# Weight sums of a Strassen product moved from GpSimd into accumulating 1 MB DMAs, with other orders of the seven products

## The chip, the cores and the metric

The kernel runs on one core of a Trainium2 chip. A core has five engines with an instruction queue each: TensorE (PE in the rows, PEld for its weight loads), VectorE (DVE), ScalarE (ACT), GpSimd (POOL) and SyncE (SP). They work at the same time and wait for one another on semaphores; each takes its own instructions in order. SP, ACT and POOL also issue DMAs, which 16 DMA engines carry out. Matmul results go to PSUM, eight banks of 128 x 512 floats; everything else lives in SBUF. The metric is the time of one execution on the device, in microseconds.

## The reference

One layer of a hybrid backbone over 1024 latent tokens and 256 context tokens of width 1024. A token mixer (long convolution, gated linear attention, gated delta net) ends in an output projection, and a squared-ReLU MLP follows:

```python
y, yc = mixer(h, hc, rows, with_ctx_out, w_in[l], w_out[l], ...)   # ends in ... @ w_out
x = x + g1 * y
x = x + g2 * sq_relu_mlp(modulate(x, norm2_g[l], sh2, sc2), w_mlp1[l], w_mlp2[l])

def sq_relu_mlp(h, w1, w2):
    return jnp.square(jax.nn.relu(h @ w1)) @ w2
```

Here w_out is 1024 x 1024, w1 1024 x 4096 and w2 4096 x 1024, all float32. A last RMSNorm gives the output.

## The kernel before

The change concerns the last part of the program: the product with w_out and the MLP, whose 4096 inner columns are worked in four quarters g, each a product with a quarter of w1 and one with a quarter of w2. That makes nine products of 1024 x 1024 weights with 1024 tokens. I call each a stage; they follow one another as w_out, w1 (g = 0), w2 (g = 0), w1 (g = 1) and so on. The stages are numbered 0 to 8, so the odd ones are w1, the even ones from 2 on are w2.

Each stage (`stage`) is one step of Strassen's scheme in Winograd's form: weights and tokens are cut into 2 x 2 blocks of 512, and seven products of blocks replace eight. The products have numbers, and `order` gives their order: (1, 5, 2, 6, 7, 4, 3) for w_out and (1, 2, 6, 7, 4, 5, 3) for the MLP. Weight blocks a11, a12, a21, a22 are combined by `weights`: a11 - a21 (product 7), a21 + a22 (5), their combinations with a11 and a12 (6 and 3). Token blocks b11 to b22 are combined by `in_place` (w_out, w2, whose inputs may be overwritten) and `apart` (w1, whose input is needed again).

Float32 operands are split into a high part that TensorE takes at full rate and a low rest (`split`): a cast on ACT makes the high part, a subtraction the low one. `operand` does that for weights into tiles S (four buffers, low part on POOL) and for tokens into tiles T (ten buffers, low part on DVE). Each matmul of operands is three matmuls (`mm3`): 4 parts p x 4 blocks k x 3 = 48 per product and 336 per stage.

Products that share a term accumulate in one PSUM bank: 6, 7 and 4 go on from 1, and 3 from 5 where 3 comes last. Before the next of them may add to a bank, `take` has read it: for w_out and w2, DVE adds the bank times a gate to x1 (the `x` tiles, `adder`); for w1, ACT and DVE form the squared ReLU in tiles `ar` (`up`).

The weights of a stage come by 16 SP transfers of 256 KB into 16 tiles `wr` that are used again stage after stage. POOL makes four sums of 128 x 512 for each p, 16 a stage.

The engines' orders are made when the program is built, by a scheduler that takes the order of the code as priority; what they are is shown below for the places that matter.

Of the kernel before, what the change touches and what calls it, by code (L numbers as in the profile page):

```python
# [119 lines left out]
def layout(x, c, ctx, c_ctx, norm1_g, norm2_g, w_mod, b_mod, w_in, w_out, hy_conv_w, hy_conv_b, hy_f_w1, hy_f_b1, hy_f_w2, hy_f_b2,  # L120
# [16 lines left out]
    A["wout"] = np.ascontiguousarray(w_out[0].reshape(8, 128, 8, 128).transpose(2, 1, 0, 3)).reshape(8, 128, 1024)  # L137
    A["w1"] = np.ascontiguousarray(w_mlp1[0].reshape(8, 128, 32, 128).transpose(2, 1, 0, 3)).reshape(32, 128, 1024)
    A["w2"] = np.ascontiguousarray(w_mlp2[0].reshape(4, 8, 128, 8, 128).transpose(0, 3, 2, 1, 4)).reshape(4, 8, 128, 1024)
# [64 lines left out]
FINAL_AT = (5, 1)  # L204
# [3 lines left out]
class Build:  # L208
# [99 lines left out]
    def run(self):  # L308
        tc, nc = self.tc, self.nc
        self._cst, self.y, self.nT = {}, [], 0  # L310
# [148 lines left out]
    def mod_rest(self, psum, pool):  # L459

        for g in (1, 2):
            yield from self.mod_group(g, psum, "psd", pool, ("mw", "mw"))
        self.stt(self.A2, self.modT[:, 32:40, 0], 1.0, self.vec("n2"), ADD, MUL)
        self.show("modT", self.modT)
        yield
# [997 lines left out]
    def weights(self, srcs):  # L1463

        gp = self.nc.gpsimd
        a = {}
# [7 lines left out]
        done = set()  # L1474

        def get(i, p):
            a11, a12, a21, a22 = [a[p, r, c] for r in range(2) for c in range(2)]
            if i > 4 and p not in done:
                done.add(p)
                self.tt(a11, a11, a21, SUB, gp)  # L1480
                self.tt(a21, a21, a22, ADD, gp)
            src = {1: a11, 2: a12, 3: a12, 4: a22, 5: a21, 7: a11}.get(i)
            if i == 6:
                src = self.temp()
                self.tt(src, a22, a11, SUB, gp)
                self.tt(a12, a12, src, SUB, gp)
            return self.operand(self.W, "S", 4, src, gp)
        return get, lambda: load(1)

    def stage(self, srcs, order, moving, take, after=None, last=None, first=None):  # L1490


        w, rest = self.weights(srcs)
        T = {}
        paired = order[-2:] == (5, 3)
# [9 lines left out]
        rest()  # L1505
        held = {}

        def bank(i, p):

            into = (1 if i in (6, 7, 4) else 5 if i == 3 and paired else i), p  # L1510
# [4 lines left out]
        for n, i in enumerate(order):  # L1515
            if last and n == 6:

                s = [w(i, p) for p in range(4)]
                for j in range(2):
                    c = slice(256 * j, 256 * j + 256)  # L1520
                    for p in range(4):
# [4 lines left out]
                        take(i, p, ps, c)  # L1526
                        if (j, p) == LAST_AT:
                            last(slice(0, 256))
                last(c)
                break  # L1530
            for p in range(4):
# [5 lines left out]
                take(i, p, ps)  # L1537
                if p == 1 and n < 6:
                    sums(order[n + 1])
# [3 lines left out]
    def in_place(self, h, early5=False):  # L1543

        def moving(i, k):
            b11, b12, b21, b22 = h(k, 0), h(k, 1), h(k + 4, 0), h(k + 4, 1)
            if i == 5 and early5:
                t = self.temp()
                self.tt(t, b12, b11, SUB)
                return t  # L1550
            if i == 6:
                self.tt(b12, b22, b12, SUB)
                self.tt(b11, b12, b11, ADD)
            elif i == 4:
                self.tt(b21, b21, b11, SUB)
            elif i == 5:
                self.tt(b12, b22, b11, SUB)
# [3 lines left out]
    def apart(self, h):  # L1561
# [3 lines left out]
        def moving(i, k):  # L1565
            b11, t3, b21, b22 = h(k, 0), h(k, 1), h(k + 4, 0), h(k + 4, 1)
            if i == 6:
                T2[k] = self.M.tile([128, 512], F32, name="u", bufs=4)
                self.tt(T2[k], t3, b11, ADD)
                return T2[k]  # L1570
            if i in (4, 5):
                t = self.temp()
                self.tt(t, b21 if i == 4 else b22, T2[k], SUB)
                return t
            return {1: b11, 2: b21, 3: b22, 7: t3}[i]
        return moving

    def adder(self, gate, acc=None, paired=True):
# [22 lines left out]
        def take(i, p, ps, s=slice(0, 512)):  # L1601
# [10 lines left out]
            elif i == 4:  # L1612
                add(ps, n, 0)
                full(n, 0)
# [24 lines left out]
    def w_out(self):  # L1639
        nc, M = self.nc, self.M  # L1640

        def load():
            self.x1 = [M.tile([128, L], F32, name=f"x1_{k}") for k in range(8)]
            for m in range(8):
# [3 lines left out]
        W = self.I["wout"]  # L1648
        self.stage([(W[p], W[p + 4]) for p in range(4)], (1, 5, 2, 6, 7, 4, 3), self.in_place(y, True), self.adder(16, self.acc, False),
                   (*NORM_AT, lambda: self.norm2(0)), None, load)  # L1650
# [32 lines left out]
    def mlp(self):  # L1683
        nc, M, x1 = self.nc, self.M, self.x1
        h = lambda k, c: self.H[k][:, 512 * c:512 * c + 512]
        order = (1, 2, 6, 7, 4, 5, 3)
        for g in range(4):
            b = {}
            new = lambda: M.tile([128, 512], F32, name="ar", bufs=16)

            def square(o, ps):

                self.act(o, ps, AF.Relu)
                self.stt(o, ps, 0.0, o, MAX, MUL)

            def up(i, p, ps):
                n = p + 4
                at = {1: (p, 0), 6: (p, 1), 7: (n, 1), 4: (n, 0)}.get(i)
                if at:
                    b[at] = new()  # L1700
                if i in (1, 6, 7):
                    nc.scalar.copy(b[at], ps)
                elif i == 4:
                    square(b[at], ps)
                elif i == 5:
                    self.tt(b[n, 1], b[n, 1], ps, ADD)
                    self.act(b[n, 1], b[n, 1], AF.Relu)
                    self.act(b[n, 1], b[n, 1], AF.Square)
                else:
                    o = b[p, 0] if i == 2 else b[p, 1]  # L1710
                    self.tt(ps, o, ps, ADD)
                    square(o, ps)
            W = self.I["w1"]
# [20 lines left out]
```

## Time and profile before

| | us |
|---|---|
| median of three runs | 1757.75 (1752.26 to 1757.88) |
| the profiled execution | 1746.09 |
| its span, first to last instruction | 1744.3 |
| of it TensorE busy | 1545.1 (89%) |
| VectorE busy | 1334.2 (76%) |
| GpSimd busy | 907.7 (52%) |
| ScalarE busy | 808.1 (46%) |

A busy share is an average over a program with many kinds of stages. PEclk is the share of the full 2.4 GHz that TensorE was granted; its lower level is 1.2 GHz. A wait is put down to the instruction whose semaphore came last. Times in the rows count from the span's start.

### The profile page before, as it was taken

The numbers are of one execution on the slowest core, as the hardware profiler recorded it, in microseconds if no ns is written. First come the engines' busy times: TensorE is split into PE (matmuls) and PEld (weight loads), VectorE is DVE, ScalarE is ACT, GpSimd is POOL, SyncE is SP. The second block draws the span as 40 slices with busy tenths as digits, with TensorE's granted clock in tenths as the row PEclk, the third lists the DMA queues.
The fourth block names the chain that finished last, engine by engine and source line by source line (L and its number), as shares of the span: only waits on it lengthen the run. The fifth ranks groups of instructions, "written<-read, shape, count | busy, mean of one in ns | idle before, by whom it ended". The sixth has DMA issues, their size and how long they took to land.

```text
span 1744.3 us, 26573 instructions
## 1 busy us (share of the span) xinstructions
PE 1545.1 (89%) x10096; PEld 1233.0 (71%) x10096; DVE 1334.2 (76%) x1820; ACT 808.1 (46%) x1468; POOL 907.7 (52%) x606
## 2 busy tenths in 40 slices
PE   7899999999999987587887997979998998899887
PEld 2487877776787766487875775768776877687766
DVE  5944597985663866879878788885898589858886
ACT  5432223245656445346542474534543454345444
POOL 0311232415244301627445695877886788678864
PEclk9999999999998977788898998989998999899988
DMA  8333876655675313345365101111111111111002
GB/s 282 123 103 117 300 287 221 226 192 182 184 217 163 127 44 111 90 155 156 108 209 188 60 14 55 43 42 55 55 42 45 53 59 39 48 49 64 34 0 97
DMA packets 123511, 202.31 MB, mean 116 GB/s; under 512 B 29943, under 2 KB 75431, under 8 KB 120696
## 3 DMA queue, kind: packets, MB, share of 16 engines
q1 hardware_dynamic: 99048, 154.45, 26.7%
q10 hardware_dynamic: 19712, 24.14, 4.5%
q0 software_dynamic: 4624, 22.02, 3.8%
q8 instruction: 80, 1.31, 0.3%
q14 instruction: 47, 0.39, 0.1%
HBM read 158.83 MB, written 41.75 MB: 115 GB/s over the span
## 4 chain that ended last, share of the span: by engine, by line
PE 28%; DVE 24%; POOL 4%; issue 3%; ACT 3%; DMA 2%; SPq 1%; POOLq 0%; ACTq 0%; DVEq 0%
PE psb L220 22%; DVE T L248 7%; DVE ar L248 5%; PE pss L220 2%; PE psl L220 2%; DVE lv L248 2%; DVE x L256 2%; POOL S L248 1%; DVE h L248 1%; DVE s L248 1%; DVE bd L248 1%; PE psi L220 1%; POOL wr L248 1%; DVE ar L256 1%; DMA h<-dy 1%
## 5 line engine op out<-in xcount | busy, mean ns | idle before, releaser
L220 PE MATMUL psb<-T,S 128*128 128x512 f32 (+1 forms) x3072 | 726.7, 398 | 80.8 <-ACT S L288 37.1
L220 PEld LDWEIGHTS psb<-T,S 128*128 128x128 f32 x3072 | 585.2, 194 | 220.5 <-ACT S L288 46.7
L248 POOL TENSOR_TENSOR S<-wr,S 128x512 fp32r<-128x512 f32 x216 | 322.8, 1500 | 183.4 <-ACT S L288 182.6
L288 ACT CAST S<-wr 128x512 fp32r<-128x512 f32 x216 | 133.2, 621 | 135.2 <-PE psb L220 115.5
L220 PE MATMUL psb<-ahi,wh 128*128 128x512 f32 x448 | 183.2, 410 | 9.1 <-DVE acc L256 4.8
L220 PE MATMUL psb<-alo,wh 128*128 128x512 f32 x448 | 181.9, 406 | 0.0
L220 PE MATMUL psb<-ahi,wl 128*128 128x512 f32 x448 | 181.0, 404 | 0.0
L248 POOL TENSOR_TENSOR wl<-ws,wh 128x1024 fp32r<-128x1024 f32 x28 | 71.1, 2539 | 206.4 <-ACT wh L288 140.8
L256 DVE SCALAR_TENSOR_TENSOR x<-psb,modT,x 128x512 f32<-128x512 f32 (+1 forms) x148 | 106.1, 727 | 57.3 <-PE psb L220 56.2
L248 DVE TENSOR_TENSOR T<-ar,T 128x512 fp32r<-128x512 f32 x112 | 135.7, 1234 | 17.6 <-ACT T L288 17.5
L256 DVE SCALAR_TENSOR_TENSOR acc<-psb,vecs,acc 128x504 f32<-128x504 f32 (+5 forms) x168 | 111.3, 678 | 49.0 <-ACT acc L260 46.7
L248 POOL TENSOR_TENSOR wr<-wr 128x512 f32<-128x512 f32 x72 | 113.7, 1581 | 12.8 <-DMA wr<-in_wout 12.2
L220 PEld LDWEIGHTS psb<-ahi,wh 128*128 128x128 f32 x448 | 87.1, 195 | 39.3 <-issue 9.1
L248 DVE TENSOR_TENSOR T<-h,T 128x512 fp32r<-128x512 f32 x88 | 107.6, 1251 | 7.8 <-ACT T L288 7.8
L288 ACT CAST T<-ar 128x512 fp32r<-128x512 f32 x112 | 68.5, 618 | 97.1 <-DVE ar L248 52.6
L220 PEld LDWEIGHTS psb<-alo,wh 128*128 128x128 f32 x448 | 87.2, 195 | 25.6 <-issue 7.8
L220 PEld LDWEIGHTS psb<-ahi,wl 128*128 128x128 f32 x448 | 87.2, 195 | 22.3 <-issue 5.1
L248 DVE TENSOR_TENSOR ar<-ar 128x512 f32<-128x512 f32 x64 | 93.2, 1471 | 0.3
L248 POOL TENSOR_TENSOR bd<-lv,qT 64x1024 f32<-64x1024 f32 x16 | 48.7, 3047 | 44.1 <-PE pss L220 32.4
L288 ACT CAST T<-h 128x512 fp32r<-128x512 f32 x88 | 53.4, 618 | 18.4 <-PE psb L220 11.4
L248 POOL TENSOR_TENSOR S<-s,S 128x512 fp32r<-128x512 f32 x36 | 55.4, 1549 | 11.9 <-ACT S L288 11.9
L248 POOL TENSOR_TENSOR s<-wr 128x512 f32<-128x512 f32 x36 | 59.5, 1663 | 1.9 <-DVE T L248 1.9
(330 smaller groups left out, 2809.5 us busy)
## 6 DMA issues: line engine op xcount, KB each, us to landing
wr<-in_w SPq DMA_DIRECT2D x128, 256.0 KB, 2.6
mw<-in_wmod SPq DMA_DIRECT2D x32, 512.0 KB, 5.2
ws<-in_win SPq DMA_DIRECT2D x28, 512.0 KB, 4.1
dft<-in_fw POOLq DMA_DIRECT2D x8, 1024.0 KB, 5.9
dft<-in_iv POOLq DMA_DIRECT2D x8, 1024.0 KB, 6.4
kq<-dKQ SPq DMA_DIRECT2D x64, 96.0 KB, 2.7
wl<-in_wmod SPq DMA_DIRECT2D x8, 512.0 KB, 3.8
wh<-in_wmod SPq DMA_DIRECT2D x8, 512.0 KB, 4.4
```

The costliest lines, as they stand in the source:

```text
L220: return self.nc.tensor.matmul(out, lhsT=lhsT, rhs=rhs, start=start, stop=stop, skip_group_check=more)
L248: return (eng or self.nc.vector).tensor_tensor(out, a, b, op)
L256: return (eng or self.nc.vector).scalar_tensor_tensor(out, a, s, b, op0=op0, op1=op1)
L288: self.nc.scalar.copy(hi, src)
```

## The change

A weight block is now a quarter of the stage's weights in one piece: 128 x 2048 floats, 1 MB, laid out so in device memory. A tile holds a whole block and serves all four p. Sums of blocks are made by issuing a second DMA from POOL into the same tile with `accum_op=ADD`, so that the transfer adds. Such a DMA can only add; therefore the second block row of the result is computed with its sign turned, which makes every weight sum a plain addition (a11 + a21, a21 + a22, a11 + a21 + a22, a11 + a12 + a21 + a22), and the sign comes back in the gates (a multiplication by -1 in `mod_rest`), in the ReLU's scale and in the token sums (`minus`). Transfers cannot subtract again, so a tile only gains blocks: `PLANS` says which blocks go into which of a stage's four or five tiles, with the products that use it in between. The tiles stand in four rooms of 1 MB, each given to the tile whose room was free first (`rooms`).

The order of the MLP's products becomes (1, 5, 6, 3, 2, 7, 4), O1, in the stages of g = 1 to 3; g = 0 keeps its order, O2, and w_out its own, O3. Since 4 now comes last in the last stage, the two final norms swap halves.

```diff
-FINAL_AT = (5, 1)
+FINAL_AT = (4, 1)
+O1, O2, O3 = (1, 5, 6, 3, 2, 7, 4), (1, 2, 6, 7, 4, 5, 3), (1, 5, 2, 6, 7, 4, 3)
+PLANS = {O1: (((0, 0), 1, (1, 0), 7), ((1, 0), (1, 1), 5, (0, 0), (0, 1), 3), ((1, 0), (1, 1), (0, 0), 6), ((0, 1), 2), ((1, 1), 4)),
...
-        def load(j):
-            for i in (j, 1 - j):
-                for p in range(4):
-                    a[p, i, j] = (self.W, self.M)[j].tile([128, 512], F32, name="wr", bufs=8)
-                    self.nc.sync.dma_start(a[p, i, j], srcs[p][i][:, 512 * j:512 * j + 512])
-        load(0)
...
+        def further(t):
+            while todo[t] and not isinstance(todo[t][0], int):
+                i, j = todo[t].pop(0)
+                if t in tiles:
+                    gp.dma_start(tiles[t], src[:, i, j, :], accum_op=ADD)
+                else:
+                    used = base + order.index([x for x in PLANS[order][t] if isinstance(x, int)][-1])
+                    room = min(self.rooms, key=self.rooms.get)
+                    self.rooms[room] = used
+                    tiles[t] = (self.W if room < 2 else self.M).tile([128, 2048], F32, name=f"wr{room}", bufs=1)
+                    self.nc.sync.dma_start(tiles[t], src[:, i, j, :])
+            if todo[t]:
+                at[todo[t].pop(0)] = t
+        def begin(n):
+            for t in sorted(range(5), key=lambda t: order.index(first(t))):
+                if t < len(todo) and t not in tiles and order.index(first(t)) <= n:
+                    further(t)
...
         def get(i, p):
-            a11, a12, a21, a22 = [a[p, r, c] for r in range(2) for c in range(2)]
-            if i > 4 and p not in done:
-                done.add(p)
-                self.tt(a11, a11, a21, SUB, gp)
-                self.tt(a21, a21, a22, ADD, gp)
-            src = {1: a11, 2: a12, 3: a12, 4: a22, 5: a21, 7: a11}.get(i)
-            if i == 6:
-                src = self.temp()
-                self.tt(src, a22, a11, SUB, gp)
-                self.tt(a12, a12, src, SUB, gp)
-            return self.operand(self.W, "S", 4, src, gp)
+            return self.operand(self.W, "S", 4, tiles[at[i]][:, 512 * p:512 * p + 512], gp)
...
+        begin_w(1 if first else 0)
         sums(order[0])
...
         for n, i in enumerate(order):
+            begin_w(n + 2)
...
                 take(i, p, ps)
+                if p == 3:
+                    used(i)
                 if p == 1 and n < 6:
                     sums(order[n + 1])
...
+            if order == O1:
+                if i == 5:
+                    self.tt(b11, b11, b12, SUB)
+                elif i == 6:
+                    self.minus(b11, b11, b22)
+                elif i == 7:
+                    self.tt(b12, b22, b12, SUB)
+                elif i == 4:
+                    self.minus(b21, b11, b21)
+                return {1: b11, 5: b11, 6: b11, 3: b22, 2: b21, 7: b12, 4: b21}[i]
...
-            if i == 6:
-                T2[k] = self.M.tile([128, 512], F32, name="u", bufs=4)
-                self.tt(T2[k], t3, b11, ADD)
-                return T2[k]
+            if i in (4, 5, 6) and k not in T2:
+                T2[k] = self.minus(self.M.tile([128, 512], F32, name="u", bufs=4), t3, b11)
             if i in (4, 5):
-                t = self.temp()
-                self.tt(t, b21 if i == 4 else b22, T2[k], SUB)
-                return t
+                return self.minus(self.temp(), T2[k], b21 if i == 4 else b22)
```

The engines' orders show what moves. On POOL, in the first half of stage 4 (w2, g = 1), before: `wr_115..` and `wr_116..` are quarter blocks, `s_...` is a temporary, and the S rows are low parts.

```order
L248 TENSOR_TENSOR S_11630<-wr_11586,S_11630 128x512
L248 TENSOR_TENSOR wr_11586<-wr_11586,wr_11594 128x512
L248 TENSOR_TENSOR S_11647<-wr_11588,S_11647 128x512
L248 TENSOR_TENSOR wr_11594<-wr_11594,wr_11614 128x512
L248 TENSOR_TENSOR s_11800<-wr_11614,wr_11586 128x512
L248 TENSOR_TENSOR wr_11588<-wr_11588,wr_11596 128x512
L248 TENSOR_TENSOR S_11676<-wr_11590,S_11676 128x512
L248 TENSOR_TENSOR wr_11596<-wr_11596,wr_11616 128x512
```

In the same place of the changed program POOL's queue reads as follows, `wr_11438` being the tile of products 1 and 7, `wr_11452` that of 5 and 3, `wr_11455` that of 6; DMASW and DMAHW are landings of DMAs issued by POOL and by SP.

```order
L255 TENSOR_TENSOR S<-wr_11438,S 128x512 [waits DMAHW5_49,PE_49,Activation_49]
L255 TENSOR_TENSOR S<-wr_11438,S 128x512 [waits PE_49,Activation_49] x3
L1487 DMA wr_11438<-in_w 128x2048 [waits Pool_49]
L255 TENSOR_TENSOR S<-wr_11452,S 128x512 [waits DMASW5_49,Activation_49]
L255 TENSOR_TENSOR S<-wr_11452,S 128x512 [waits Activation_49] x3
L1487 DMA wr_11452<-in_w 128x2048 [waits Pool_49]
L255 TENSOR_TENSOR S<-wr_11455,S 128x512 [waits DMASW7_49,Activation_49]
L255 TENSOR_TENSOR S<-wr_11455,S 128x512 [waits Activation_49]
L1487 DMA wr_11452<-in_w 128x2048 [waits DMASW1_49]
L255 TENSOR_TENSOR S<-wr_11455,S 128x512 [waits Activation_49] x2
L255 TENSOR_TENSOR S<-wr_11452,S 128x512 [waits DMASW2_49,Activation_49]
```

The sums between the low parts are gone; in their place stand DMA issues, of which the second into `wr_11452` waits for the landing of the first, and product 3's first low part for the landing of the second.

On DVE at the border of stage 3 (w1) and stage 4 (w2), before: `x1_...<-psb` rows are the adds of product 1, the rows of `ar` from `ar` alone token sums for product 6, the T row a low part for product 6.

```order
L256 SCALAR_TENSOR_TENSOR x1_0_8914<-psb_11633,modT_156,x1_0_8914 128x512
L256 SCALAR_TENSOR_TENSOR ar_11244<-psb_11498,ar_11244 128x512
L248 TENSOR_TENSOR ar_11030<-ar_11222,ar_11030 128x512
L256 SCALAR_TENSOR_TENSOR x1_1_8915<-psb_11650,modT_156,x1_1_8915 128x512
L248 TENSOR_TENSOR ar_11244<-ar_11332,ar_11244 128x512
L248 TENSOR_TENSOR ar_11405<-ar_11405,ar_11030 128x512
L248 TENSOR_TENSOR ar_11048<-ar_11244,ar_11048 128x512
L256 SCALAR_TENSOR_TENSOR x1_2_8916<-psb_11679,modT_156,x1_2_8916 128x512
L248 TENSOR_TENSOR ar_11423<-ar_11423,ar_11048 128x512
L248 TENSOR_TENSOR T2_11756<-ar_11030,T2_11756 128x512
```

The same border in the changed program, where T8 and T9 belong to product 5 and T0 to T3 to product 6:

```order
L255 TENSOR_TENSOR T8_11502<-ar_10911,T8_11502 128x512
L255 TENSOR_TENSOR T9_11506<-ar_10929,T9_11506 128x512
L263 SCALAR_TENSOR_TENSOR ar_10911<-ar_10911,ar_10996 128x512
L255 TENSOR_TENSOR T0_11579<-ar_10847,T0_11579 128x512
L263 SCALAR_TENSOR_TENSOR ar_10929<-ar_10929,ar_11014 128x512
L263 SCALAR_TENSOR_TENSOR ar_11435<-psb_10916,ar_11435 128x512
L255 TENSOR_TENSOR T1_11583<-ar_10865,T1_11583 128x512
L263 SCALAR_TENSOR_TENSOR x1_0_8905<-psb_11462,modT_156,x1_0_8905 128x512
L263 SCALAR_TENSOR_TENSOR x1_1_8906<-psb_11479,modT_156,x1_1_8906 128x512
L263 SCALAR_TENSOR_TENSOR x1_2_8907<-psb_11512,modT_156,x1_2_8907 128x512
```

The token sums now stand ahead of product 1's adds, not among them.

## Rows read from the trace of the kernel before

**Rows 1.** The core's span in us and its mean granted TensorE clock.

```profile
core 0: 1744.3 us, clock 0.933
```

**Rows 2.** Stages: length, busy of PE, PEld, DVE, ACT, POOL; clock, DMA, GB/s.

```profile
916.80:1018.00 101.20, 86.33 (x355) 69.31 (x354) 82.03 (x96) 41.73 (x73) 65.33 (x43) 0.91 0.30 109
1018.00:1114.30 96.30, 82.80 (x354) 65.51 (x353) 83.96 (x89) 61.00 (x108) 69.63 (x47) 0.95 0.14 44
1114.30:1207.40 93.10, 82.24 (x338) 66.07 (x337) 74.38 (x74) 35.49 (x60) 68.21 (x46) 0.93 0.14 45
...
1286.40:1380.90 94.50, 81.89 (x338) 65.33 (x337) 75.23 (x76) 35.47 (x60) 69.06 (x46) 0.95 0.13 45
1380.90:1460.10 79.20, 77.03 (x338) 62.73 (x337) 63.67 (x62) 46.02 (x85) 65.50 (x44) 1.00 0.17 54
...
1633.90:1731.40 97.50, 85.57 (x404) 70.75 (x402) 81.29 (x94) 43.84 (x78) 64.58 (x43) 0.93 0.06 22
1731.40:1744.30 12.90, 2.75 (x15) 2.19 (x14) 5.24 (x14) 1.64 (x6) 4.19 (x6) 0.59 0.48 163
```

**Rows 3.** Timeline of TensorE in stage 5: start, length, what, idle before.

```profile
1414.39 47.88 PE L220 MATMUL psb<-T,S 128*128 128x512 f32 x209 [0.82 <-ACT S L288]
```

**Rows 4.** Timeline of TensorE in the first half of stage 4.

```profile
1310.16 15.72 PE L220 MATMUL psb<-T,S 128*128 128x512 f32 x60 [4.76 <-ACT S L288]
1332.38 9.85 PE L220 MATMUL psb<-T,S 128*128 128x512 f32 x31 [6.50 <-DVE x L256]
```

**Rows 5.** Chain of waits from 1280 to 1345 us, summed by line.

```profile
by line: DVE ar L248 35.3%; DVE T L248 29.8%; PE psb L220 19.7%; DVE x L256 9.2%; DVE ar L256 3.8%; DVE psb L248 3.7%; ACT ar L260 0.9%; issue 0.4%
```

**Rows 6.** Busy times from 1280 to 1332 us, columns as in rows 2.

```profile
1280.00:1332.00 52.00, 39.77 (x163) 30.74 (x161) 51.27 (x46) 16.89 (x30) 50.87 (x31) 0.96 0.05 16
```

**Rows 7.** DVE and ACT on `ar`: count, then shortest, median, longest ns.

```profile
L248 DVE TENSOR_TENSOR T<-ar,T x112: 677/1217/1785, 1093.5 to 1707.6; 128x512 fp32r<-128x512 f32 x112
...
L256 DVE SCALAR_TENSOR_TENSOR ar<-psb,ar x48: 672/678/693, 1053.3 to 1647.5; 128x512 f32<-128x512 f32 x48
```

**Rows 8.** DVE groups, 1280 to 1332 us: count, busy us, mean ns, idle.

```profile
L248 DVE TENSOR_TENSOR ar<-ar 128x512 f32<-128x512 f32 x16 | 23.8, 1501 | 0.1
L248 DVE TENSOR_TENSOR T<-ar,T 128x512 fp32r<-128x512 f32 x13 | 20.1, 1563 | 0.0
```

**Rows 9.** POOL's weight sums, whole run, columns as in rows 8.

```profile
L248 POOL TENSOR_TENSOR wr<-wr 128x512 f32<-128x512 f32 x72 | 113.7, 1581 | 12.8 <-DMA wr<-in_wout 12.2
...
L248 POOL TENSOR_TENSOR s<-wr 128x512 f32<-128x512 f32 x36 | 59.5, 1663 | 1.9 <-DVE T L248 1.9
L248 POOL TENSOR_TENSOR wr<-wr,s 128x512 f32<-128x512 f32 x36 | 57.8, 1608 | 0.0
```

**Rows 10.** 1 MB loads issued by POOL: issue ns; us to landing.

```profile
L1365 POOL DMA_DIRECT2D dft<-in_fw x8: 528/554/583, 191.8 to 299.6; - x8
...
DMA to landing us min/median/max: 5.0/6.0/12.6
```

**Rows 11.** Groups on POOL from 1280 to 1332 us.

```profile
L248 POOL TENSOR_TENSOR wr<-wr 128x512 f32<-128x512 f32 x8 | 13.6, 1696 | 0.1
L248 POOL TENSOR_TENSOR s<-wr 128x512 f32<-128x512 f32 x4 | 6.9, 1746 | 0.0
L248 POOL TENSOR_TENSOR wr<-wr,s 128x512 f32<-128x512 f32 x4 | 6.9, 1731 | 0.0
```

**Rows 12.** Timeline of POOL in stage 0.

```profile
923.38 1.45 POOL L248 TENSOR_TENSOR wr<-wr 128x512 f32<-128x512 f32 x1 [10.31 <-DMA wr<-in_wout]
```

**Rows 13.** Timeline of TensorE in stage 0.

```profile
932.65 14.28 PE L220 MATMUL psb<-T,S 128*128 128x512 f32 x48 [4.05 <-ACT S L288]
```

**Rows 14.** The casts and low parts of S: shortest, median, longest ns.

```profile
L288 ACT CAST S<-wr x216: 602/622/647, 896.3 to 1721.6; 128x512 fp32r<-128x512 f32 x108
L248 POOL TENSOR_TENSOR S<-wr,S x216: 1260/1398/1832, 897.0 to 1722.3; 128x512 fp32r<-128x512 f32 x108
```

More of the change, by code (lines that the diff above doesn't have):

```diff
@@ L309, in run @@
         tc, nc = self.tc, self.nc
-        self._cst, self.y, self.nT = {}, [], 0
+        self._cst, self.y, self.nT, self.nS, self.rooms = {}, [], 0, 0, {i: i - 9 for i in range(4)}
         with ExitStack() as es:
@@ L1461, in temp, with weights @@
         return self.M.tile([128, 512], F32, name="s", bufs=2)
[L1463 removed]
+    def weights(self, src, order):
         gp = self.nc.gpsimd
[L1466 to L1488 removed]
@@ L1490, in stage @@
-    def stage(self, srcs, order, moving, take, after=None, last=None, first=None):
-        w, rest = self.weights(srcs)
+        at, todo, tiles = {}, [list(t) for t in PLANS[order]], {}
+        base = 8 * self.nS
+        self.nS += 1
+        def further(t):
[11 more added lines that the diff above has]
+                at[todo[t].pop(0)] = t
@@ new lines, in begin, with first @@
+        def begin(n):
+            for t in sorted(range(5), key=lambda t: order.index(first(t))):
+                if t < len(todo) and t not in tiles and order.index(first(t)) <= n:
+                    further(t)
+        def first(t):
+            return next(x for x in PLANS[order][t] if isinstance(x, int)) if t < len(todo) else order[0]
+        def get(i, p):
+            return self.operand(self.W, "S", 4, tiles[at[i]][:, 512 * p:512 * p + 512], gp)
+        return get, begin, lambda i: further(at[i])
@@ L1494, in stage @@
+    def stage(self, src, order, moving, take, after=None, last=None, first=None):
+        w, begin_w, used = self.weights(src, order)
         T = {}
-        paired = order[-2:] == (5, 3)
         def sums(i):
@@ L1504, in stage @@
             first()
-        rest()
         held = {}
         def bank(i, p):
-            into = (1 if i in (6, 7, 4) else 5 if i == 3 and paired else i), p
+            into = (1 if i in (6, 7, 4) else 5 if i == 3 and order != O3 else i), p
             begin = into not in held
@@ L1526, in stage @@
                         take(i, p, ps, c)
+                        if after and j == 0 and (i, p) == after[:2]:
+                            after[2]()
                         if (j, p) == LAST_AT:
@@ L1541, in stage, with minus, in_place @@
                     after[2]()
-    def in_place(self, h, early5=False):
+    def minus(self, out, a, b):
+        self.stt(out, a, -1.0, b, MUL, SUB)
+        return out
+    def in_place(self, h, order):
         def moving(i, k):
             b11, b12, b21, b22 = h(k, 0), h(k, 1), h(k + 4, 0), h(k + 4, 1)
-            if i == 5 and early5:
+            if order == O1:
[8 more added lines that the diff above has]
+                return {1: b11, 5: b11, 6: b11, 3: b22, 2: b21, 7: b12, 4: b21}[i]
+            if i == 5 and order == O3:
                 t = self.temp()
-                self.tt(t, b12, b11, SUB)
+                self.tt(t, b11, b12, SUB)
                 return t
@@ L1612, in take @@
             elif i == 4:
-                add(ps, n, 0)
-                full(n, 0)
+                add(ps, n, 0, s)
+                full(n, 0, s)
             elif i == 5:
@@ L1647, in w_out @@
         y = lambda k, c: self.y[k][:, 512 * c:512 * c + 512]
-        W = self.I["wout"]
-        self.stage([(W[p], W[p + 4]) for p in range(4)], (1, 5, 2, 6, 7, 4, 3), self.in_place(y, True), self.adder(16, self.acc, False),
-                   (*NORM_AT, lambda: self.norm2(0)), None, load)
+        self.stage(self.I["wout"][0], O3, self.in_place(y, O3), self.adder(16, self.acc, False), (*NORM_AT, lambda: self.norm2(0)), None, load)
     def norm2(self, c):
```

57 lines of the change are left out of this document (31 added, 26 removed).

## The prediction

> **What bounds the kernel now.** I read the clock and span first [rows 1], then a table of busy time by stage, then the chain of waits and the instruction groups in the worst stretch, last the DMA landings. The last 827.5 us of the span are nine matrix products (w_out, then w1 and w2 four times), each in seven Strassen products; I cut them at every 336th matmul into T and S. The reader should see in [rows 2] two kinds of stage: a w1 stage lasts 79.2 us with the clock at 1.00 (2.4 GHz), a w2 stage 93.1 to 97.5 us at 0.93 to 0.95. An undisturbed run of 209 matmuls takes 47.88 us [rows 3], 0.229 us each, so a product of 48 costs 11.0 us and a stage 77. The first two stages, 101.2 and 96.3 us, have troubles of their own. All the rest of the program (the first 917 us) keeps its order but for neighbours that swap.
>
> The 15.3 us by which a w2 stage (94.5) exceeds a w1 stage are two idle gaps of TensorE, 4.76 and 6.50 us, one ended by a cast of S on ACT, one by an x add on DVE [rows 4], and some 5 us more of busy time (81.9 against 77.0) under the lower clock. In the stretch of those gaps the chain of waits lies 82% on DVE (35.3 + 29.8 + 9.2 + 3.8 + 3.7) [rows 5]. There, in 52 us, DVE is busy 51.27 us with 46 instructions and POOL 50.87 us with 31 [rows 6]. DVE is slow, not only full: a TENSOR_TENSOR with both operands in SBUF takes 0.677 us at best, 1.217 in the median and 1.785 at worst, while the form with one operand in PSUM takes 0.672 to 0.693 whatever POOL does [rows 7]; in the stretch the 29 SBUF ones average 1.50 and 1.56 us [rows 8]. Two-operand SBUF work on DVE and work on POOL take turns.
>
> **The change, part by part.**
>
> *POOL's sums go.* 72 + 36 + 36 instructions of 1.58 to 1.66 us, 231 us of POOL in all [rows 9], are replaced by 50 accumulating transfers (4 + 2 x 5 + 6 x 6). POOL issues 1 MB loads already, in 0.53 to 0.58 us [rows 10]: 50 x 0.57 = 28 us, hidden by what went. In the 52 us stretch 8 + 4 + 4 = 16 of POOL's 31 instructions are such sums [rows 11], 15 remain. If each remaining one holds up one DVE instruction by 0.85 us (1.53 - 0.68), DVE needs 29 x 0.68 + 17 x 0.70 + 15 x 0.85 = 44.4 us; bounds are 51.3 (every instruction still slow) and 31.6 (none). TensorE needs 163 x 0.229 = 37.3 for its matmuls there, so relief alone gives 6.9 us and leaves 7.1.
>
> *Order of the products.* DVE's work is the same in number: 16 sums in a w2 stage, 12 in a w1 stage, now partly SCALAR_TENSOR_TENSOR, whose row reads 0.678 with one PSUM operand [rows 7]; with two SBUF operands I take the same 0.68, and if POOL slows it as it does the others that is already in the 0.85. In the order 1,5,6,3,2,7,4 the sums for product 5 need nothing of the previous stage's last product, and the x add of product 1 stands behind the last sum instead of among them; two other products lie between 6 and the next accumulation into its bank, where before there was none. That should hide 5 of the 7.1 us; I keep 2 (bounds 0 and 7). So a w2 stage in the new order comes to 79.2 + 2 = 81.2, a gain of 13.3, and the clock stays up because the gaps go. Three such stages: -40. The w2 stage that keeps the old order gets the relief and 1 us of clock: -8 (0 to -13). The three w1 stages in the new order put eight DVE instructions in front of product 5, of which the order shows four to six made a stage earlier: +1.5 each, +4.5 (-2 to +8 each at the bounds: 77 is the floor, the eight cost at most 8 x 1.0 us).
>
> *First two stages.* In w_out POOL waited 10.31 us for a load before its sums [rows 12] and TensorE 4.05 us for the S that followed [rows 13]. Now two whole megabytes are loaded first and added on the way: -5 (0 to -8). The w1 stage behind it keeps its order and gets POOL's relief: -4 (0 to -8).
>
> *The transfers.* A stage loads 4 MB now at a DMA share of 0.17 [rows 2]; then 5 plain and 6 accumulating megabytes. Counting an accumulating one twice, 17/4 x 0.17 = 0.72: room enough, if each lands in time. Tiles follow a chain: the tile of products 5 and 3 gets two additions between them, the second waiting on POOL for the landing of the first, and behind it in POOL's queue stand the low parts of S for product 6. Time from the start of a stage: with S four deep, the last S of product 5 is split when TensorE ends product 1, 11.0 + 0.62 + 1.40 [rows 14] = 13.0; first addition issued by 13.6; second at 14.2 + L; product 3 begins at 33.0 and its first S needs 2.0 behind the landing. So 14.2 + 2L + 2.0 <= 33: nothing is lost up to L = 8.4 us, and 2L - 16.8 us per stage beyond. ACT's casts of T queue behind the same S, and so would be late too. The tile of product 6 gets two additions beside product 4 of the stage before; by the same count POOL's wait there is free up to L = 9.2 us in three stages and 11.9 in three, then costs the excess. Six stages have this order; in the other two orders the chains have a product or more to spare.
>
> L is in no row. Below it is a lone 1 MB load from POOL, 5.0 us; above, the latest of such loads, 12.6 us, taken with a second one under way [rows 10]. An accumulating megabyte reads two and writes one, between one load and two; I take 8 us, an estimate nearer to the median load (6.0) plus a read than to the pair, and so no stall. At 12.6 the price is 6 x 8.4 + 3 x 3.4 + 3 x 0.7 = 63 us.
>
> The Trainium skill (Collectives: The Full Stack, "The bandwidth ceiling: the fold count and why AG ≠ RS ≠ AR") says that adding in the DMA path halves the rate, since each chunk needs two source reads through one ring. No run here shows an accumulating DMA. By that rule a whole landing doubled would be the most, which is the third rival below.
>
> *Ends.* Two TENSOR_SCALAR of four columns, the gate's sign: nothing. The tail behind the last matmul, 12.9 us [rows 2], treats the other half of the columns in the same way: nothing.
>
> Sum: -40 - 8 + 4.5 - 5 - 4 = -52.5. Against the profiled execution, 1746.1 us (span 1744.3), that is 1693.6; the median of the runs is 11.7 above that execution, so I predict **1705 us** for a median.
>
> **Rivals.**
> *Slow additions (slower).* If an accumulating megabyte takes 12 us or more, TensorE waits before product 3 in each of the six stages; from about L = 12 the loss (6 x 7.2 + 3 x 2.8 + 0.3 = 52) eats the gain, at 12.6 it is 1768, at 14 it is -52.5 + 67 + 21 = +36, 1793. For it: the 12.6 us landing, and a chain of five steps per tile through one in-order queue. Against it: in these stages hardly another transfer is under way.
> *DVE stays the bound.* POOL's S parts remain, 252 of them, and DVE meets them in lockstep; then a w2 stage keeps 8 of its 15.3 us, -7 each: -21 - 3 + 4.5 - 4 = -23.5, 1734. For it: DVE busy 51 of 52 us; against: half of POOL's work in that stretch goes.
> *Doubled landing.* Reading the tile as well as the weights takes as long again as a lone load [rows 10], L = 2 x 5.0 = 10.0: 6 x 3.2 + 3 x 0.8 = 22 us back, -31, 1727. For it: nothing in the rows says that the two reads overlap. Against it: part of the 5.0 us is fixed, whatever is moved, and is not paid twice. It is what the rule of the Trainium skill named above comes to here at most.
> *No net change.* L just about 11.5 to 12.2, or the new order's own stalls as large as the old: 1757.
>
> **How the numbers follow.** Forecast 0.48, its own range 1684 to 1728 (w2 stages at 79 to 84, w1 stages at 77 to 82); better than that 0.04; doubled landing 0.10; DVE bound 0.10; no change 0.06; slow additions 0.22. A measurement of this kernel tells about 0.3%, 5 us, from nothing. Faster: 0.48 + 0.04 + 0.10 + 0.10 = 0.72; within 0.06; slower 0.22. The range 1682 to 1782 leaves out some 0.04 below and 0.12 above (L past 13.4).
>
> **What would show it.** Right: w2 stages at 79 to 84 us with the clock at 1.00, DVE's T<-ar median below 1.0 us, POOL at some 45 us busy per stage, additions landing under 8.4 us, TensorE not waiting for a cast of S at the start of product 3. Wrong: POOL or ACT idle ended by a DMA on wr with TensorE idle behind it, landings of 12 us or more (slow additions), or gaps ended by DVE x as before (DVE bound). A w1 stage over 84 us would mean that the sums for product 5 came late.

## The result and the profile after

| | before | after |
|---|---|---|
| median of the runs, us | 1755.01 (1747.72 to 1757.88, 4 runs) | 1687.13 (1682.12 to 1693.78, 4 runs) |
| the profiled execution, us | 1746.09 | 1693.78 |

The ratio is 0.9622, with a 95% interval of 0.957 to 0.9673. Run once more beside other kernels, the changed one came to 0.9623 (0.9594 to 0.9652). The medians differ by 68 us and the two profiled executions by 52: that of before was the fastest of its runs, that of after the slowest. The working below goes by the profiled ones, as the prediction's did.

The core's row, then the nine stages and the tail in the columns of [rows 2], and last the 52 us around the border of stages 3 and 4, to be read against [rows 6]:

```profile
core 0: 1691.9 us, clock 0.938
```

```profile
918.40:1021.80 103.40, 84.07 (x355) 66.88 (x353) 81.17 (x96) 40.44 (x71) 49.50 (x34) 0.91 0.55 156
1021.80:1114.70 92.90, 82.31 (x352) 66.75 (x353) 71.83 (x90) 61.76 (x110) 44.91 (x34) 0.93 0.45 109
1114.70:1198.80 84.10, 79.33 (x338) 65.05 (x337) 66.72 (x77) 35.53 (x60) 43.55 (x34) 0.96 0.57 136
1198.80:1279.70 80.90, 77.58 (x337) 63.48 (x336) 60.52 (x69) 47.21 (x88) 44.09 (x34) 0.99 0.58 133
1279.70:1356.60 76.90, 76.90 (x337) 63.61 (x336) 58.86 (x69) 33.98 (x57) 43.91 (x35) 0.99 0.65 164
1356.60:1438.90 82.30, 78.77 (x338) 63.89 (x338) 60.59 (x67) 46.65 (x87) 44.20 (x34) 0.98 0.57 130
1438.90:1515.00 76.10, 76.10 (x337) 63.02 (x336) 60.87 (x71) 34.52 (x58) 42.54 (x34) 1.00 0.63 159
1515.00:1593.20 78.20, 76.78 (x338) 62.88 (x337) 53.13 (x62) 44.85 (x85) 41.13 (x34) 1.00 0.59 141
1593.20:1676.80 83.60, 80.89 (x405) 67.62 (x403) 68.81 (x85) 41.76 (x79) 47.79 (x34) 1.00 0.33 72
1676.80:1691.90 15.10, 2.95 (x13) 2.38 (x12) 6.84 (x18) 1.63 (x5) 4.89 (x7) 0.63 0.69 248
1273.00:1325.00 52.00, 49.29 (x211) 40.27 (x210) 45.16 (x49) 24.86 (x44) 31.38 (x25) 0.97 0.59 142
```

Three things are to be seen. The w2 stages in the new order came down (76.9, 76.1, 83.6); in the first two of them TensorE is busy from end to end. The w1 stages 3 and 5 became longer (80.9, 82.3), and stage 0 did too (103.4). DVE has 45.16 us of work in the 52, against 51.27 before. The chain of waits from 1275 to 1345 us, by line, is TensorE's own where 82% of it was DVE's [rows 5]:

```profile
by line: PE psb L227 98.0%; POOL S L255 2.2%; issue 0.1%
```

The instructions of DVE on `ar` (count, then shortest, median, longest ns; compare [rows 7]):

```profile
L255 DVE TENSOR_TENSOR T<-ar,T x112: 673/682/5071, 1094.0 to 1656.4; 128x512 fp32r<-128x512 f32 x112
L263 DVE SCALAR_TENSOR_TENSOR ar<-ar x36: 671/679/6122, 1110.8 to 1636.1; 128x512 f32<-128x512 f32 x36
```

The median of the low parts of T fell from 1217 to 682 ns; but the longest rose from 1785 to 5071, and a token sum once took 6122. Before, nothing of the kind lasted longer than 1.8 us. The page's section of DMA issues has the two kinds of weight load (KB each, median us from issue to landing):

```profile
wr<-in_w POOLq DMA_DIRECT2D x46, 1024.0 KB, 8.1
wr<-in_w SPq DMA_DIRECT2D x40, 1024.0 KB, 5.0
```

POOL's issues of them, by line (shortest, median, longest ns):

```profile
L1487 POOL DMA_DIRECT2D wr<-in_w x46: 870/882/900, 1001.2 to 1619.1; - x46
```

So a landing takes about what the prediction took, 8 us; an issue takes 0.88 us, not 0.57. What that does at the end of stage 3 stands in three timelines (start, length, what, idle before), first POOL's, then DVE's, then TensorE's:

```profile
1265.70 0.88 POOL L1487 DMA_DIRECT2D wr<-in_w  x1 [1.07 <-DMA wr<-in_w]
1267.81 1.29 POOL L255 TENSOR_TENSOR S<-wr,S 128x512 fp32r<-128x512 f32 x1 [1.23 <-ACT S L295]
1274.21 0.88 POOL L1487 DMA_DIRECT2D wr<-in_w  x1 [5.11 <-DMA wr<-in_w]
1274.81 5.27 POOL L255 TENSOR_TENSOR S<-wr,S 128x512 fp32r<-128x512 f32 x4
```

```profile
1274.51 0.68 DVE L263 SCALAR_TENSOR_TENSOR ar<-psb,ar 128x512 f32<-128x512 f32 x1
1275.11 5.54 DVE L255 TENSOR_TENSOR ar<-ar 128x512 f32<-128x512 f32 x1
1280.57 0.68 DVE L263 SCALAR_TENSOR_TENSOR ar<-ar 128x512 f32<-128x512 f32 x1
```

```profile
1264.83 8.89 PE L227 MATMUL psb<-T,S 128*128 128x512 f32 x38 [0.61 <-DVE ar L255]
1276.44 18.94 PE L227 MATMUL psb<-T,S 128*128 128x512 f32 x75 [2.71 <-POOL S L255]
```

POOL stands 5.11 us before the second addition into the tile of product 6, for the landing of the first. Four low parts of S queue behind it; ACT had cast the first of them by 1270.8. TensorE waits 2.71 us for that one. And the four run in one go, while a DVE sum that would take 0.68 us is held for 5.54, to the end of that run.

### The profile page after: what moved, and what is told of

The parts are those of the page before. It is cut to its first block, busy times and chain, and to the rows that moved or that the text cites. A ratio compares the mean times of both kernels' runs of the same rounds, so it can differ in the third digit from the quotient of the medians.

```text
span 1691.9 us, 26193 instructions
## 1 busy us (share of the span) xinstructions
PE 1525.0 (90%) x10096; PEld 1222.7 (72%) x10096; DVE 1256.2 (74%) x1822; ACT 802.1 (47%) x1468; POOL 706.6 (42%) x512
## 4 chain that ended last, share of the span: by engine, by line
PE 56%; DVE 23%; DMA 8%; ACT 5%; issue 4%; POOL 2%; ACTq 0%; SPq 0%; POOLq 0%; DVEq 0%
PE psb L227 42%; PE pss L227 8%; DVE lv L255 4%; DVE T L255 3%; DMA wr<-in_w 3%; PE psl L227 2%; DVE hb L255 2%; POOL S L255 1%; PE psi L227 1%; DVE x L263 1%; DVE ar L263 1%; PE psd L227 1%; DVE acc L263 1%; DVE bd L255 1%; DVE acc L255 1%
## 5 line engine op out<-in xcount | busy, mean ns | idle before, releaser
L227 PE MATMUL psb<-T,S 128*128 128x512 f32 (+1 forms) x3072 | 708.0, 392 | 45.1 <-POOL S L255 12.4
L227 PEld LDWEIGHTS psb<-T,S 128*128 128x128 f32 x3072 | 577.3, 191 | 173.9 <-POOL S L255 16.7
L255 POOL TENSOR_TENSOR S<-wr,S 128x512 fp32r<-128x512 f32 x252 | 364.2, 1488 | 296.6 <-ACT S L295 288.2
L295 ACT CAST S<-wr 128x512 fp32r<-128x512 f32 x252 | 154.3, 619 | 174.3 <-PE psb L227 91.0
L255 DVE TENSOR_TENSOR T<-h,T 128x512 fp32r<-128x512 f32 x88 | 94.9, 1107 | 69.1 <-ACT T L295 68.7
L255 DVE TENSOR_TENSOR T<-ar,T 128x512 fp32r<-128x512 f32 x112 | 118.8, 1086 | 10.8 <-ACT T L295 10.8
L1487 POOL DMA_DIRECT2D wr<-in_w x46 | 40.6, 882 | 66.6 <-DMA wr<-in_w 53.0
L267 ACT ACTIVATE acc<-psb,vecs 128x512 f32<-128x512 f32 (+1 forms) x48 | 31.1, 662 | 63.8 <-PE psb L227 29.8
L267 ACT ACTIVATE ar<-psb 128x512 f32<-128x512 f32 x48 | 28.7, 598 | 47.4 <-DVE psb L255 42.6
```

What stands on the lines that cost most here:

```text
L227: return self.nc.tensor.matmul(out, lhsT=lhsT, rhs=rhs, start=start, stop=stop, skip_group_check=more)
L255: return (eng or self.nc.vector).tensor_tensor(out, a, b, op)
L267: return self.nc.scalar.activation(out, a, f, bias=bias, scale=scale)
L295: self.nc.scalar.copy(hi, src)
L1487: gp.dma_start(tiles[t], src[:, i, j, :], accum_op=ADD)
```

## The experiments

Twelve runs, each compared with the kernel before on the same chip: the changed kernel (`after`) once more, and ten variants of it, one of them twice. Three of the variants (no additions, a third addition, plain transfers) compute wrong sums and only tell times.

| kernel | median, us | ratio to before (95%) |
|---|---|---|
| after, again | 1686.21 | 0.9623 (0.9594 to 0.9652) |
| old order of the products, transfers kept | 1696.22 | 0.9684 (0.9647 to 0.972) |
| new order, sums on POOL | 1695.53 | 0.9677 (0.9654 to 0.9701) |
| no additions | 1651.57 | 0.943 (0.9407 to 0.9453) |
| a third addition | 1737.68 | 0.9916 (0.9889 to 0.9942) |
| plain transfers instead of additions | 1659.44 | 0.9469 (0.9436 to 0.9502) |
| second addition for product 6 later | 1689.05 | 0.9634 (0.96 to 0.9668) |
| stage 2 in another order | 1689.31 | 0.9638 (0.9607 to 0.967) |
| x loads on SP | 1674.68 | 0.9556 (0.9512 to 0.9601) |
| x loads on SP, again | 1674.95 | 0.9554 (0.9522 to 0.9586) |
| that, and half of S's low parts on DVE | 1651.9 | 0.9441 (0.9411 to 0.9471) |
| that, and all of them on DVE | 1647.63 | 0.9408 (0.9376 to 0.9439) |

**The old order with the new transfers.**

```diff
-            order = O1 if g else O2
+            order = O2
```

(The final norms' halves swap back with it.)

> The accumulating transfers with the order of the kernel before (1, 2, 6, 7, 4, 5, 3) in all eight MLP stages; everything is still computed. My theory (relief of VectorE and the new order each do a part): the w2 stages 4, 6 and 8 go back from 76.9, 76.1 and 83.6 us to 84 to 88, as stage 2 has, which kept that order, and the w1 stages 3, 5 and 7 fall back to about 79; in all some 18 us over the changed kernel, 1705 us. Rival 1 (the order does all of it): w2 stages at 93 or more, 1740. Rival 2 (the transfers do all of it, the order nothing): 1687.

Stages 4 and 5:

```profile
1273.40:1357.30 83.90, 78.56 (x337) 64.01 (x336) 66.55 (x76) 35.25 (x60) 43.63 (x34) 0.98 0.52 129
1357.30:1433.50 76.20, 76.20 (x337) 63.07 (x337) 55.90 (x63) 47.22 (x85) 44.35 (x33) 1.00 0.56 137
```

The w2 stages came out at 84 to 87 as expected, but all three w1 stages at 76.2 or 76.3, not 79: there the transfers gain and the new order loses. So beside the transfers the order gives 9 to 10 us in all, not 18.

**The new order with the sums on POOL.** In `weights`, 16 quarter tiles and four sums for each p, one each for products 5, 6, 3 and 7 in the order of the lines:

```diff
-                    gp.dma_start(tiles[t], src[:, i, j, :], accum_op=ADD)
...
+            if name == "a":
+                self.tt(a21, a21, a22, ADD, gp)
+            elif name == "b":
+                self.tt(a11, a11, a21, ADD, gp)
+            elif name == "c":
+                o = a21 if order == O1 else a12
+                self.tt(o, a11, a12, ADD, gp)
+            else:
+                self.tt(a11, a11, a22, SUB, gp)
```

> The new orders and signs, but the weight sums on GpSimd again, 16 of 128 x 512 a stage (in place, on 16 quarter tiles), no accumulating transfer; everything is still computed. My theory: VectorE stays slow beside GpSimd, its T low parts keep a median of about 1.2 us, and only the order helps, 5 to 7 us in each of the three w2 stages: about 1740. Rival 1 (the order does all of it): about 1695. Rival 2 (the order does nothing): 1755.

My theory missed by 45 us; the number is that of the first rival (1695). Stage 2 (old order), stage 4, and the 52 us around the border of stages 3 and 4:

```profile
1115.50:1198.30 82.80, 79.33 (x338) 63.82 (x337) 73.70 (x77) 35.51 (x60) 69.72 (x46) 0.98 0.18 51
1275.30:1357.70 82.40, 79.47 (x338) 62.22 (x337) 73.36 (x71) 35.57 (x60) 73.32 (x49) 1.00 0.18 52
...
1273.00:1325.00 52.00, 49.07 (x203) 37.05 (x202) 51.47 (x47) 23.17 (x41) 49.98 (x31) 1.00 0.12 34
```

DVE's low parts of T in the same kernel:

```profile
L255 DVE TENSOR_TENSOR T<-ar,T x112: 673/1218/1786, 1096.0 to 1659.5; 128x512 fp32r<-128x512 f32 x112
```

DVE is as slow as before (median 1218 ns against 1217) and as full (51.47 of 52 us against 51.27 in [rows 6]), with POOL at 49.98; yet stage 4 takes 82.4 us instead of 94.5 with the clock at 1.00, and TensorE is busy 49.07 us of the 52 against 39.77. The full DVE was not in itself what stopped TensorE; it mattered what stood behind what. One thing this kernel does not separate: its four sums are spread over products 5, 6, 3 and 7 instead of standing in one block before product 6, and stage 2, which keeps the old order of products, fell as well, from 93.1 to 82.8, nearly as much as stage 4. So the first rival (the order of the products does all of it) is not shown by its number: the placing of POOL's sums has a part in it, perhaps most, and how much is open.

**No additions at all.**

```diff
-                    gp.dma_start(tiles[t], src[:, i, j, :], accum_op=ADD)
+                    pass
```

> The changed kernel without the 50 accumulating transfers: each tile keeps its first block, so the sums of weight blocks are left out of the computation. Tells what the additions cost at all. My theory: only what they make TensorE wait for, that is some 5 us in the last products of stages 3 and 5, 1.5 us in stage 7 and up to 5 in stage 0: 1675 to 1682. Rival (the additions slow VectorE, GpSimd or the other loads through and through): 1665 or less, with the T low parts clearly under their 0.68 us median share of slow ones and w1 stages at 77.

The rival was nearer. Every stage from 2 to 7 takes 76.3 us from its first matmul to its last, whatever its order, and no DVE instruction on `ar` takes over 1.8 us. Stage 4:

```profile
1252.40:1328.60 76.20, 76.20 (x338) 63.09 (x337) 56.60 (x70) 34.81 (x58) 37.67 (x29) 1.00 0.20 70
```

So the additions cost the changed kernel 35 us, where I expected 5 to 12. They do so in two places. Stages 2 to 8 are 26 us shorter here than in the first profile of the changed kernel and 24 shorter than in its second; stage 0, at 89.5, is 14 and 9 us shorter.

**A third addition.**

```diff
-PLANS = {O1: (... ((1, 0), (1, 1), 5, (0, 0), (0, 1), 3), ...
+PLANS = {O1: (... ((1, 0), (1, 1), 5, (0, 0), (0, 1), (0, 1), 3), ...
```

> A third addition (the block a12 a second time, so the weights of product 3 are wrong by it) in the tile of products 5 and 3, between those two products, in the six stages of the new order. My theory (the chain of landings has no slack left: 14.2 us, then L each, then 2.0): each of the six stages becomes some 8 us longer, with TensorE idle before product 3, about 48 us in all, 1735 us. Rival (the two landings still have slack, as the landings are hidden by products 5 and 6): under 15 us more, 1700 at most.

It took 51 us more than the changed kernel. TensorE in stage 4, at product 3:

```profile
1299.80 14.35 PE L227 MATMUL psb<-T,S 128*128 128x512 f32 x62
1323.04 7.24 PE L227 MATMUL psb<-T,S 128*128 128x512 f32 x23 [8.90 <-ACT S L295]
```

The six stages grew by 5.5, 10.3, 6.4, 11.8, 8.0 and 7.1 us, 49 in all. The prediction's count for this chain (14.2 + L each + 2.0) holds in the mean: two landings of 8 us just fit, a third does not.

**Plain transfers in their place.**

```diff
-                    gp.dma_start(tiles[t], src[:, i, j, :], accum_op=ADD)
+                    gp.dma_start(tiles[t], src[:, i, j, :])
```

> The 50 accumulating transfers as plain ones from the same queue, at the same places and with the same waits: each overwrites its tile, so the sums of blocks are wrong. Without any addition the kernel took 1651.6 us, 35 us less than the changed kernel. Theory A (those 35 us are the landings of 8 us, for which GpSimd and product 3 wait): landings fall to about 5 us and most comes back, 1655 to 1662. Theory B (they come from the issue on GpSimd: each VectorE instruction longer than 2.5 us begins just after such an issue and ends with GpSimd's run of S low parts): about 14 such long ones remain, with the gap of 4.8 us before product 7 of stage 2, and 1670 or more. I give B 0.6.

It was theory A, to which I gave less. The issues by line, and their landings:

```profile
L1487 POOL DMA_DIRECT2D wr<-in_w x46: 568/568/592, 996.4 to 1580.7; - x46
...
DMA to landing us min/median/max: 5.0/5.2/11.0
```

And the low parts of T:

```profile
L255 DVE TENSOR_TENSOR T<-ar,T x112: 673/681/2601, 1084.2 to 1618.1; 128x512 fp32r<-128x512 f32 x112
```

With landings of 5.2 us instead of 8.0 and the same queue, places and waits, stages 2 to 7 are at 76.3 again; a single DVE instruction exceeds 2.5 us, where the changed kernel has 14. So 28 of the 35 us hang on the adding itself (the longer landing and issue, which are not separated here), some 7 or 8 on the rest.

**The second addition for product 6 later.** A sum of one column on POOL, which needs the second S of product 1, holds it back:

```diff
+            self.tt(self.tiny, tiles[2][:, 0:1], s[:, 1, 0:1].bitcast(F32), ADD, gp)
+            further(2)
...
```

> The second addition into the tile of product 6 is held back by a 128 x 1 sum on GpSimd until the second S of product 1, in the six stages of the new order, so that GpSimd no longer waits for a landing in the product before. Everything is computed. My theory (the 4.8 and 6.1 us by which stages 3 and 5 exceed 76.3 come from that wait and the run of four S low parts after it): stages 3 and 5 at 77 to 78, 1678 us in all. Rival (any issue that meets a queue of S low parts shuts VectorE out, wherever it stands): the gap goes into product 1 or 5 of the next stage, 1687.

Both were right in part. Stages 3 and 4:

```profile
1196.00:1273.20 77.20, 76.50 (x337) 62.97 (x337) 56.43 (x67) 45.45 (x86) 41.67 (x32) 1.00 0.60 145
1273.20:1352.50 79.30, 76.94 (x337) 62.85 (x336) 65.58 (x71) 34.69 (x60) 50.31 (x39) 1.00 0.63 151
```

Stage 3 fell from 80.9 to 77.2, and stage 4 rose from 76.9 to 79.3, with TensorE idle in product 6. In sum nothing: 1689 against 1686 and 1687. The wait moved.

**Stage 2 in another order.**

```diff
-O1, O2, O3 = (1, 5, 6, 3, 2, 7, 4), (1, 2, 6, 7, 4, 5, 3), (1, 5, 2, 6, 7, 4, 3)
+O1, O2, O3, O4 = (1, 5, 6, 3, 2, 7, 4), (1, 2, 6, 7, 4, 5, 3), (1, 5, 2, 6, 7, 4, 3), (1, 2, 5, 6, 3, 7, 4)
...
-            order = O1 if g else O2
+            order, order2 = (O1, O1) if g else (O2, O4)
...
-            self.stage(self.I["w2"][g], order, self.in_place(lambda k, c: b[k, c], order), ...
+            self.stage(self.I["w2"][g], order2, self.in_place(lambda k, c: b[k, c], order2), ...
```

> Stage 2 (w2, g = 0) alone in the order 1, 2, 5, 6, 3, 7, 4 instead of 1, 2, 6, 7, 4, 5, 3. Everything is computed. My theory (the old order leaves product 7 right behind product 6 in one bank, and a late add of 6 stops TensorE): the gap of 4.8 us before product 7 goes, the clock stays up, stage 2 falls from 84.1 to 77 to 78, about 1680. Rival (VectorE is shut out beside the same issues in any order): the gap stands before another product, 1687.

Stages 2 and 3:

```profile
1115.90:1195.00 79.10, 76.51 (x338) 62.93 (x337) 66.73 (x74) 34.20 (x59) 44.50 (x34) 1.00 0.67 161
1195.00:1278.70 83.70, 78.76 (x337) 64.41 (x336) 65.41 (x74) 47.22 (x88) 46.96 (x36) 0.96 0.59 135
```

Stage 2 gained 5.0 us and stage 3 lost 2.8. Product 7's gap (the first row, of the changed kernel) went, and one came before product 5 (the second row, of this one):

```profile
1152.28 4.18 PE L227 MATMUL psb<-T,S 128*128 128x512 f32 x9 [4.77 <-DVE x L263]
1140.39 1.86 PE L228 MATMUL psb<-T,S 128*128 128x512 f32 x7 [2.59 <-DVE x L264]
```

The total is unchanged within what the runs can tell, as the rival said.

**The loads of x on SP.**

```diff
-                nc.scalar.dma_start(self.x1[m], self.I["xT"][m])
+                nc.sync.dma_start(self.x1[m], self.I["xT"][m])
```

> The eight loads of x (512 KB each) in stage 0 issued by SyncE instead of ScalarE. Everything is computed. My theory (ScalarE's queue stands 18.4 us in these issues, so the casts of T and S for product 5 come 8 us late): the gap of 8.6 us before product 5 of stage 0 goes, stage 0 at 95 to 98 instead of 103.4, about 1680. Rival (the tile of product 5 is itself late, its two blocks landing at some 927 to 937 us in a full DMA): the gap stays, 1687.

In the changed kernel ACT's queue stands in these issues, and a cast of T waits behind them:

```profile
915.99 18.42 ACTq L1681 DMA_DIRECT2D x<-in_xT  x6
934.46 1.66 ACT L295 CAST T<-h 128x512 fp32r<-128x512 f32 x3 [18.94 <-DMA x<-in_xT]
```

With them on SP the gap of 8.63 us before product 5 is gone:

```profile
922.90:1007.90 85.00, 81.56 (x355) 66.69 (x354) 72.02 (x96) 42.96 (x73) 44.20 (x34) 0.97 0.65 190
```

Stage 0 takes 85.0 us, where I expected 95 to 98; in the two profiles of the changed kernel it takes 103.4 and 98.3. But it begins 4 us later (at 922.9, against 918.4 and 919.2), so that its end comes some 14 and 10 us earlier. The second run, beside the changed kernel, confirms 11 us of the median. What was expected of these two:

> The loads of x on SyncE once more: 12 us under the changed kernel beside it, 1672 to 1678 us, if the gain seen in three rounds is real; within 5 us of it if not.

> The changed kernel once more, unaltered, for the comparison with the three next to it: 1682 to 1694 us as before.

**The low parts of S on DVE.**

```diff
-            return self.operand(self.W, "S", 4, tiles[at[i]][:, 512 * p:512 * p + 512], gp)
+            return self.operand(self.W, "S", 4, tiles[at[i]][:, 512 * p:512 * p + 512], None)
```

(In the half version `gp if p % 2 else None`; both with x on SP.)

> The loads of x on SyncE, and of the low parts of S those of even p on VectorE instead of GpSimd. Everything is computed. Theory (VectorE is shut out for a whole run of GpSimd's low parts that begins with an issue): the runs halve, no VectorE instruction over 3.2 us stays, half of the 5 us per stage that the additions still cost goes: 1660 to 1668. Rival (VectorE's extra 14 x 0.68 = 9.5 us a stage and its waits for landings cost more than that): 1675 or more.

> The loads of x on SyncE, and all low parts of S on VectorE, GpSimd only issuing in these stages. Everything is computed. Theory (two-operand work of VectorE is slow only beside GpSimd's): T low parts and token sums all at 0.67 to 0.70 us, VectorE at some 70 of 76 us in a w2 stage, stages 3 to 7 at 76.3 to 78, the total 1650 to 1660. Rival (VectorE becomes the bound, being 70 of 76 us busy and standing in order behind landings): w2 stages at 80 or more, 1680 and up.

Both theories held in the main, and more came back than they said: 1651.9 us, where I expected 1660 to 1668, and 1647.63, where I expected 1650 to 1660. With all on DVE, stages 4 and 5:

```profile
1246.30:1323.60 77.30, 76.67 (x337) 62.90 (x336) 61.22 (x96) 34.36 (x58) 5.20 (x6) 1.00 0.63 151
...
1323.60:1399.80 76.20, 76.20 (x338) 63.07 (x337) 59.47 (x98) 47.83 (x88) 5.20 (x6) 1.00 0.64 152
```

And there the low parts of T:

```profile
L255 DVE TENSOR_TENSOR T<-ar,T x112: 679/686/694, 1072.7 to 1608.0; 128x512 fp32r<-128x512 f32 x112
```

DVE does 27 to 31 instructions more per stage than in the changed kernel and is busy 61.22 us instead of 58.86 in stage 4, 59.47 instead of 60.59 in stage 5; POOL is left with 5.2 us of issues of its 44 us, and the low parts that DVE took over cost it nearly nothing, because none of T's on `ar` takes over 0.7 us any more. I had expected some 70 us of DVE in a w2 stage. Landings still take 8.0 us in the median: POOL waits for them with nothing behind it. In the half version two DVE instructions of 3.5 and 3.7 us remain, where I expected none over 3.2. The full version, at 1647.63 us, is 39 us below the changed kernel run beside it (11 of them the x loads), and by its median the fastest kernel that computes everything.

## Why the prediction was right, and which of its steps were not

It gave 1705 us for the median, between 1682 and 1782, and 1693.6 for an execution like the profiled one; the profiled one took 1693.8. That agreement is luck: the execution profiled was the slowest of four, the changed kernel's second profile comes from one of 1686.64, and the median, 1687.13, lies 18 us under the forecast. The sum is better than its parts, too, whose errors cancel (lengths after less those before):

| term | predicted, us | measured, us |
|---|---|---|
| three w2 stages in the new order | -40 | -50 |
| w2 stage in the old order | -8 | -9.0 |
| three w1 stages in the new order | +4.5 | +4 |
| stage 0 | -5 | +2 |
| stage 1 | -4 | -3.4 |
| before the stages, and the tail | 0 | +4 |

*POOL's sums go.* Right in what it does to DVE: 45.16 us busy in the stretch, where 44.4 were worked out, though with luck: the sum has 15 instructions held by 0.85 us each, and in the trace two that lasted 5.54 and 3.06 us make half of what goes beyond 0.68. Wrong was the step from there to TensorE, "relief alone gives 6.9 us and leaves 7.1", of which the order hides 5. The two halves do not add up. Transfers alone bring 56 us of the 66 to 68, and the new order with sums on POOL, otherwise placed, 57, with DVE as slow and full as before. Alone, the one takes 10.6 and the other 12.1 us out of stage 4. Both together reach the floor of TensorE in stages 4 and 6, which is 76.2 and not the 81.2 that I kept.

*The w1 stages.* The size is right by accident. I charged DVE's eight sums before product 5. They cost nothing: with the additions left out, the same order runs in 76.2. The cost is POOL's wait for product 6's tile beside the last product of the stage before, which I held to be free "up to L = 9.2 us in three stages". At 8.2 it cost stage 3, with 80.9 us, most of 4.7: a gap of 2.71, and soon behind it five matmuls that follow one another at 0.43 us instead of 0.23. With the second addition held back the stage took 77.2. My count began that chain too early: the plain load into the room was issued at 1258.86 and took 6.31 us, so the first addition went out at 1265.70 and the second at 1274.21.

*The additions.* L at 8.0 is right, though it was only a choice between 5.0 and 12.6, and so is the chain between products 5 and 3 (in stage 7, where two successive landings took 9.01 and 8.74 us, 2L - 16.8 gives 0.95, and TensorE waited 0.80 and 0.62 at product 3). The Trainium skill (Collectives: The Full Stack, "The bandwidth ceiling: the fold count and why AG ≠ RS ≠ AR") speaks of a halved rate where the DMA path adds in a collective; here a landing takes 8.0 us where the same transfer without adding takes 5.2, a factor of 1.55. The rival built on a doubled landing falls with it. But "no stall" was taken for "no cost". Additions cost 35 us, as the kernel without them shows. Some 25 of them lie in stages 2 to 8: POOL stands in order behind a landing, a run of low parts gathers, and DVE is shut out of it; with those low parts on DVE the same additions leave these stages at 76.2 to 79.2, almost as without any. The others lie in the main in stage 0. The w2 stages' larger gain paid for all that.

*Stage 0.* That "two whole megabytes are loaded first" was right, but POOL's wait had been cover for another: ACT's 18.4 us in the issues of x. Six of the eight issues wait for loads of h and w_out, which land later beside the additions: the sixth of the eight went out at 929.7, without additions at 918.1. The first two additions took 11.8 and 17.2 us to land there, which L = 8 left out. I did not say what would be late next.

*The tail.* It grew from 12.9 to 15.1 us. In the kernel with the old order everywhere it is 13.3, in that with the new order and POOL sums 14.9: it comes with the new order and its swap of the halves, not with the transfers.

Of the rivals, slow additions needed landings of 12 us; of the 46 in the MLP only one took so long (12.34). "DVE stays the bound" fell in two ways: in the changed kernel DVE is relieved, and with the sums on POOL it stays as slow and full and still does not bind.

## What to carry to other kernels

Moving work off an engine pays twice where it slows another by it (here POOL went from 69 to 44 us a stage, and DVE's low parts from 1.22 to 0.68 us), but a helper that must wait for its own transfers holds up all that stands behind it in its queue: count what gathers there and who is hurt when it runs. Before giving an engine relief, ask whether its work needs the helper at all; here one engine's work given to the other, with no contention, cost almost nothing. And an engine at 99% is not yet the bound: change the order of its work, and of what it waits for, once before you remove any.

## What the runs showed of the hardware that was not expected

Before, DVE's two-operand work and POOL's took turns: no DVE instruction of the nine stages was longer than 1.79 us. In the changed kernel 14 DVE instructions last 2.6 to 7.7 us. Each begins 0.2 to 2.2 us after POOL began to issue an accumulating transfer, and ends 0.56 us after the end of a POOL instruction, one of up to six that follow that issue without a pause, in all but one case the last of them. Instructions of DVE with one operand in PSUM do not show it (at most 0.69 us on `ar`). The Trainium skill (SBUF — State Buffer, "Who interferes with whom") says that a DVE instruction with two SBUF inputs contends with a GpSimd instruction that reads SBUF, and calls the port pair that they share an exclusive lock. The rows of before agree, with waits for about one instruction; after an issue it was a run of up to six. That it takes the run, and not the issue or the landing alone, is shown by the last kernel, which has the same issues and landings and no low parts on POOL: no DVE instruction of the nine stages exceeds 1.8 us there. That it takes the issue too is shown by the kernels without accumulating or plain ones from POOL in these stages (before, no additions, sums on POOL): none exceeds 1.87 us. A plain issue can do the same: with plain transfers three DVE instructions, of 2.60, 2.28 and 1.95 us, began within 1.1 us of one and ended 0.56 us after the one or two low parts behind it. Longer runs did not gather behind a plain issue. Why the turns stop after an issue stays open.

An accumulating megabyte costs POOL 0.88 us to issue where a plain one costs 0.57.
